# A hybrid attention layer: diagonal copies in scrow, first modulation weights in contiguous blocks, x scaled one K-tile sooner and at first out of PSUM

## The chip, the cores and the metric

The kernel runs on one core of a Trainium2 chip. The core has a matrix engine (TensorE, PE in the profile; its weight loads are the row PEld), a vector engine (VectorE, DVE), a scalar engine (ScalarE, ACT), GpSimd (POOL) and SyncE (SP), which here issues nearly all transfers between the chip's memory and SBUF, the on-chip memory. Products of TensorE land in PSUM, eight banks of 2 KB in each of 128 partitions. The metric is the device time of one execution in microseconds, the median of several runs.

## The reference

One layer with S = 512 tokens and D = 1024 channels, in float32. Cut to what matters:

```python
mod = silu(c) @ w_ada + b_ada                    # c is one vector of 1024
shift, scale, gate = split(mod, 3)
h = rms_norm(x, norm_gain) * (1 + scale) + shift # x is 512 x 1024
proj = h @ w_in                                  # q, k, v, z of head groups A and B, and gates
# group A: sliding-window attention; group B: compressed, selected and window-512 branches
y = concat(o_a * silu(z_a), o_b * silu(z_b)) @ w_out
out = x + gate * y
```

The norm divides each token by the root of its mean square over the 1024 channels. The modulation (`scale`, `shift`) is a product of a vector with a 1024 x 3072 matrix, for each of the 1024 channels.

## The kernel before, in words

**Layout.** x is held transposed, as eight K-tiles of 128 channels by 512 tokens (`xT[0]` to `xT[7]`, in one tile `xTp`). The products with `w_in` run in float32 precision through pairs of rounded parts: h is kept as a high part `hh[k]` and a low part `hl[k]`, the weights as `swh` and `swl`, and each K-tile's product is made of three (`hh` x `swh`, `hh` x `swl`, `hl` x `swh`).

**The head** (lines 312 to 401), all of it with an order written out by hand: inside `in_order` each engine runs its instructions as they stand in the text.

- SyncE issues the transfers: eight K-tiles of x (256 KB each), then for k = 0 to 3 the modulation weights `ada[k]` (1 MB each, `load_ada`), the small `bias` after the first of these, and the weight rows `wst[k]` of the first projection (384 KB each, `load_wst`); then `rest`.
- A tanh of c gives `sc_col`, the silu of c (doubled), a column per block of 128 channels. To have it as a row in all partitions, VectorE makes two diagonal tiles `diag` (128 x 512, line 341), each holding four diagonal blocks, and TensorE multiplies them by ones (line 343). ScalarE copies the two results into `scrow` (line 372) once the sums below are done.
- ScalarE squares each K-tile of x (line 363), VectorE adds the squares up in two groups of four (line 365), and TensorE sums the columns over the partitions (`sums`, line 352). The last tile is done in halves. VectorE then works out the inverse root (`rsqrt`, lines 113 to 120) and TensorE spreads it by transposes into the PSUM tile `rbp` (line 384).
- For K-tiles 0 and 1 the modulation is worked out on TensorE: `mod_pe` (line 252) multiplies the columns of `ada[k]` by c, ScalarE copies the result to `macc` (line 255), `mod_col` sums it and `mod_ab` makes AB, scale and shift of h. For K-tiles 2 to 7 VectorE does it (`mod_rows`, line 242: a multiply with `scrow` and a sum along the row, once for shift, once for scale).
- `fillers` are matmuls whose result nobody reads. The tuple `ND` says how many stand at which place.
- `scaled(k, by)` (line 292) multiplies K-tile k of x by the inverse root on VectorE. Tile 0 takes it out of PSUM (`rbp`) in two halves; the others take it out of `rb`, an SBUF copy that ScalarE makes (line 397). `h_high` makes `hh[k]` and `hf[k]` on ScalarE (line 298; 395 and 398 for tile 0), `h_low` makes `hl[k] = hf[k] - hh[k]` on VectorE (line 301). `weights_high` and `weights_low` split `wst[k]` on ScalarE (line 284) and VectorE (line 287).

**The first projection** (lines 414 to 438): for each K-tile three products (`first_proj`, lines 308 and 309) of 8 matmuls each. After the second of K-tile k, `new_tile(k + 1)` puts the work of the next tile on ScalarE and VectorE. VectorE's order in `new_tile(k)` is `mod_rows(k + 1)`, `h_low(k)`, `scaled(k + 1)`, `weights_low(k + 1)`.

**The remainder** (from 53 us): projections of the other columns, attention of both groups and the output product. Its order comes from generators that are interleaved by cost.

**Buffers.** Tiles of 128 x 512 (`T2`) come out of one pool, small constants out of `con`, PSUM tiles `pj` out of pools of 2 KB banks. The kernel is built with `auto_bufs`: a planner places the tiles in memory after the program's order is known, and may put a tile where another lay whose last reader it takes to be done; the later writer then waits for that reader. It also settles the order of instructions that no `in_order` or `block` fixes. Loads are numbered over eight semaphores, so an issue waits until the transfer eight places before it has landed.

Of the kernel before, what the change touches and what calls it, by code (L numbers as in the profile page):

```python
# [9 lines left out]
F32 = mybir.dt.float32  # L10
# [21 lines left out]
NEAR = 256  # L32
ND = (11, (0, 0, 0, 0, 1, 1, 1, 1), (2, 0), 1, 1, 0, 3)
NR = 4
# [57 lines left out]
def hybrid_layer_kernel(ctx, tc, A, out):  # L92
# [126 lines left out]
    def load_ada(k):  # L219
        t = ada_ring[:, k % NR]  # L220
        if k < PE_MODS:
            ada[k] = t.rearrange("p (a b c) -> p a b c", a=8, b=2)
            for e, n in ((0, 4), (4, 2), (6, 2)) if k == 0 else ((0, 4), (4, 4)):
                SP.dma_start(ada[k][:, e:e + n], A["w_ada_cols"][k][:, e:e + n])
        else:
            ada[k] = t.rearrange("p (a b) -> p a b", a=2)
            for e in range(2):
                SP.dma_start(ada[k][:, e], A["w_ada_rows"][k - PE_MODS][:, e])
# [83 lines left out]
    with in_order(tc) as begun:  # L312
# [8 lines left out]
        for k in range(NR):  # L321
            load_ada(k)
            if k == 0:
                SP.dma_start(bl, A["bias"])
            load_wst(k)
        SP.dma_start(rest, A["rest"])
# [12 lines left out]
        for e in range(2):  # L339
            diag = T2(F32, "diag").rearrange("p (j q) -> p j q", j=4)  # L340
            DVE.tensor_tensor(diag, ident[:, None, :].to_broadcast([128, 4, 128]),
# [35 lines left out]
        DVE.tensor_tensor(prmg[:, 0:8], prm1, prm[:, 24:32], op=OP.mult)  # L377
        DVE.tensor_scalar(prmg[:, 8:16], prm[:, 24:32], 0.5, None, op0=OP.mult)
        fillers(ND[3])
        mod_pe(0, lambda: fillers(ND[4]))  # L380
        fillers(ND[5])
        rbp = ps_pj.tile([128, 512], F32, name="pj")
# [3 lines left out]
        PE.matmul(pl, bl[:, NEAR:NEAR + 40], bl[:, 0:NEAR], start=True, stop=True)  # L386
        fillers(ND[6])
        weights_high(0)
# [10 lines left out]
        weights_low(0)  # L399
        scaled(1, rb)  # L400
        h_low(0)

        def new_tile(k):

            h_high(k, halves if k < 4 else (slice(0, S),))
            if k < 7:
                mod_rows(k + 1, (1,) if k == 1 else (0, 1))
            h_low(k)
            if k < 7:
                scaled(k + 1, rb)  # L410
                weights_high(k + 1)
# [824 lines left out]
def _layout(inp):  # L1236
# [6 lines left out]
    wa = g("w_ada")[0].reshape(8, 128, 3, 8, 128)[:, :, 0:2, 0:PE_MODS]  # L1243
    a["w_ada_cols"] = cc(wa.transpose(3, 1, 0, 2, 4))
    wr = g("w_ada")[0].reshape(D, 3, 8, 128)
# [66 lines left out]
```

## Time and profile before

| | |
|---|---|
| median of 3 runs | 301.43 us (300.99 to 306.27) |
| the profiled execution | 301.42 us |
| its span from first to last instruction | 299.1 us |
| TensorE busy | 292.2 us, 98% |
| TensorE weight loads busy | 254.6 us, 85% |
| VectorE busy | 263.6 us, 88% |
| ScalarE busy | 203.3 us, 68% |
| GpSimd busy | 10.2 us, 3% |
| read from memory, written | 41.74 MB, 2.14 MB |

Times in the rows are counted from the first instruction. A row of the timeline gives start, length, engine, line of the kernel, operation, `output<-input` by the program's names with sizes, and a count; in brackets stands how long the engine had been idle and what ended it. Rows of engines whose name ends in q are those of an engine's instruction queue, transfers' issues among them. A row of the waits gives who waited for whom, the total in us, the number of times and the longest.

### The profile page before, as it was taken

The page shows a single profiled execution, that of the slowest core. Times are in us where ns is not written, and L with a number is a line of the kernel's source. Part 1 is how long each engine was busy: PE and PEld are TensorE (multiplying, and loading weights), DVE is VectorE, ACT ScalarE, POOL GpSimd, SP SyncE. Part 2 cuts the span into 40 slices and gives each one's busy share as a digit, 9 for nine tenths or more (in the row PEclk, how much of TensorE's full clock was granted, in tenths as well). Part 3 has the DMA queues.
Part 4 walks back from the last instruction along what each step waited for, and adds up shares of the span by engine and source line. Part 5 has one row for each costly group of instructions (what it writes and reads, how often), then busy time and mean ns, then how long its engine had stood idle before and what let it go on. Part 6 is the DMA issues. An engine that isn't in the chain of part 4 may idle for free.

```text
span 299.1 us, 6080 instructions
## 1 busy us (share of the span) xinstructions
PE 292.2 (98%) x2179; PEld 254.6 (85%) x2179; DVE 263.6 (88%) x736; ACT 203.3 (68%) x498; POOL 10.2 (3%) x28
## 2 busy tenths in 40 slices
PE   8899999999999999999999999999999999999995
PEld 3678878879989899989877888888888888889995
DVE  4688998999996899899999999988989779599992
ACT  4676656886857666886839575888878769567520
POOL 1000000000000100000000000000000000021210
PEclk9999999999999999999999999999999999999999
DMA  7999975980393766526312211303200220027262
GB/s 263 356 406 358 417 277 178 309 263 2 90 343 104 247 203 216 178 70 233 117 41 71 70 37 35 140 3 114 100 0 2 69 75 0 2 40 191 53 155 92
DMA packets 26649, 44.27 MB, mean 148 GB/s; under 512 B 1867, under 2 KB 17900, under 8 KB 26620
## 3 DMA queue, kind: packets, MB, share of 16 engines
q1 hardware_dynamic: 25612, 42.49, 41.8%
q0 software_dynamic: 864, 1.31, 2.9%
q8 instruction: 17, 0.28, 0.4%
q10 hardware_dynamic: 144, 0.09, 0.1%
q14 instruction: 12, 0.10, 0.1%
HBM read 41.74 MB, written 2.14 MB: 147 GB/s over the span
## 4 chain that ended last, share of the span: by engine, by line
PE 75%; DVE 14%; ACT 5%; issue 3%; DMA 2%; SPq 1%; DVEq 0%; ACTq 0%
PE pj L499 15%; PE pj L489 9%; PE sq L308 8%; PE po L1056 8%; PE pj L1166 6%; PE s L965 5%; PE pt L1037 4%; PE skv L309 4%; PE s L1166 3%; DVE wl L193 3%; PE pt L1023 2%; PE po L499 2%; DMA xTp<-in_xT 2%; DVE kTb L567 2%; PE pt L1166 1%
## 5 line engine op out<-in xcount | busy, mean ns | idle before, releaser
L489 PE MATMUL pj<-wh,hh 128*128 128x256 f32 (+1 forms) x128 | 37.3, 291 | 0.0
L489 PE MATMUL pj<-wl,hh 128*128 128x256 f32 (+1 forms) x128 | 36.7, 286 | 0.0
L489 PE MATMUL pj<-wh,hl 128*128 128x256 f32 (+1 forms) x128 | 36.6, 286 | 0.0
L971 ACT ACTIVATE pp<-pp,nm 128x256 f32<-128x256 f32 (+2 forms) x48 | 29.2, 610 | 5.4 <-DVE nm L967 5.3
L192 ACT ACTIVATE wh<-raw 128x512 fp32r<-128x512 f32 (+1 forms) x40 | 24.8, 637 | 6.6 <-PE pj L499 4.6
L499 PE MATMUL pj<-hh,wh 128*128 128x512 f32 x72 | 28.9, 402 | 0.0
L499 PE MATMUL pj<-hl,wh 128*128 128x512 f32 x72 | 28.9, 401 | 0.0
L499 PE MATMUL pj<-hh,wl 128*128 128x512 f32 x72 | 28.7, 398 | 0.0
L193 DVE TENSOR_TENSOR wl<-raw,wh 128x512 fp32r<-128x512 f32 (+1 forms) x40 | 27.0, 692 | 0.8 <-issue 0.2
L967 DVE CUSTOM_DVE_ANT_0 pp<-s,bias 128x256 f32<-128x256 f32 (+2 forms) x48 | 25.7, 550 | 2.0 <-PE s L965 1.5
L489 PEld LDWEIGHTS pj<-wh,hh 128*128 128x128 f32 x128 | 24.1, 189 | 0.4 <-issue 0.3
L489 PEld LDWEIGHTS pj<-wh,hl 128*128 128x128 f32 x128 | 24.2, 189 | 0.2 <-issue 0.2
L489 PEld LDWEIGHTS pj<-wl,hh 128*128 128x128 f32 x128 | 24.2, 189 | 0.0
L965 PE MATMUL s<-kTb,qs 128*128 128x256 f32 (+2 forms) x96 | 23.6, 349 | 0.0
L1008 DVE TENSOR_SCALAR pp<-pp,rr,grev 128x256 f32<-128x256 f32 (+2 forms) x48 | 21.2, 474 | 0.4
L965 PEld LDWEIGHTS s<-kTb,qs 128*128 128x128 f32 x96 | 16.8, 189 | 2.4 <-issue 0.2
L1038 ACT COPY ptT<-pt 128x384 f32<-128x384 f32 (+1 forms) x32 | 15.5, 525 | 1.9 <-PE pt L1037 1.9
L971 ACT ACTIVATE pa<-pa,nm 128x129 f32<-128x129 f32 x32 | 12.7, 399 | 5.1 <-DVE nm L987 4.7
L1037 PE MATMUL pt<-first,pp 128*128 128x128 f32 x112 | 15.7, 274 | 0.0
L499 PEld LDWEIGHTS pj<-hh,wl 128*128 128x128 f32 x72 | 13.6, 189 | 2.4
L499 PEld LDWEIGHTS pj<-hl,wh 128*128 128x128 f32 x72 | 13.6, 188 | 2.2
L499 PEld LDWEIGHTS pj<-hh,wh 128*128 128x128 f32 x72 | 13.6, 188 | 2.2
(296 smaller groups left out, 835.1 us busy)
## 6 DMA issues: line engine op xcount, KB each, us to landing
ada_ring<-in_w_ada_rows SPq DMA_DIRECT2D x12, 512.0 KB, 7.7
raw<-in_w_cmp SPq DMA_DIRECT2D x8, 512.0 KB, 5.8
raw<-in_w_gate SPq DMA_DIRECT2D x8, 512.0 KB, 4.5
raw<-in_w_o SPq DMA_DIRECT2D x8, 512.0 KB, 3.4
wst_ring<-in_w_qkv_a SPq DMA_DIRECT2D x8, 384.0 KB, 8.2
xTp<-in_xT SPq DMA_DIRECT2D x8, 256.0 KB, 4.5
bias<-line_d SPq DMA_DIRECT2D x8, 256.0 KB, 3.7
raw<-in_w_q_b SPq DMA_DIRECT2D x4, 512.0 KB, 5.0
```

Of the source, the lines that this page charges most:

```text
L192: ACT.activation(wh, src, AF.Copy)
L193: DVE.tensor_tensor(wl, src, wh.bitcast(F32), op=OP.subtract)
L308: PE.matmul(pj_q[tb], lt, w[:, 0:512], start=f, stop=l, skip_group_check=True)
L489: PE.matmul(bank[:, t * n:(t + 1) * n], h[:, tb * 128:(tb + 1) * 128], w[:, k % 2, :], start=k == 0 and m == 0, stop=k == 7 and m == 2)
L499: PE.matmul(bank, w, h, start=k == 0 and m == 0, stop=k == 7 and m == 2)
L965: PE.matmul(ps, qs[8 + 4 * g + r][:, 128 * i:128 * i + 128], kT[br, g][:, hl_, 0:w], start=hl_ == 0, stop=hl_ == 1)
L967: DVE.tensor_tensor_reduce(out=P[:, g, 0:w], in0=ps, in1=bias["b", r, g][:, 512 - w:512], scale=1.0, scalar=3e38, op0=OP.add, op1=OP.min, ...
L971: ACT.activation(P[:, g], P[:, g], AF.Exp, bias=nm[:, g:g + 1], scale=-1.0, accum_out=dn[:, g:g + 1])
L1008: DVE.tensor_scalar(v, v, rr[:, g:g + 1], gates[:, g, br:br + 1], op0=OP.mult, op1=OP.mult)
L1037: PE.transpose(pt[:, b * 128:(b + 1) * 128], P[:, g, b * 128:(b + 1) * 128], ident)
L1056: PE.matmul(o[64 * g:64 * g + 64, 128 * i:128 * i + 128], vb[:, 64 * g:64 * g + 64], sl["T"][g][:, b, :], start=first_of and b == 0, stop= ...
L1166: PE.matmul(parts[g, p], a[:, r, :], b, start=new and r == 0 and m == 0, stop=r == 3 and m == 2, skip_group_check=True)
```

## The change

- The two diagonal tiles are no tiles of their own. They are written into the two halves of `scrow`, in which the result of their products is put later.
- The modulation weights of K-tiles 0 and 1 lie in memory as four blocks of 128 x 512 each, contiguous, 256 KB (before: one row of 8 KB for each partition, of which each transfer took a part). K-tile 0 comes in four transfers of one block (before: three, of 512, 256 and 256 KB), K-tile 1 in two of two blocks.
- The load of `wst[k]` is issued before that of `bias`.
- Of the fillers around `mod_pe(0)` (one ahead, one in its middle) one is left, behind it.
- K-tiles 1 and 2 of x are both scaled ahead of `h_low(0)`, out of `rbp` in PSUM. The copy `rb` stays, for the later tiles.
- In `new_tile(k)` VectorE scales K-tile k + 2 (before: k + 1), ahead of `h_low(k)` (before: behind it).

```diff
-ND = (11, (0, 0, 0, 0, 1, 1, 1, 1), (2, 0), 1, 1, 0, 3)
+ND = (11, (0, 0, 0, 0, 1, 1, 1, 1), (2, 0), 1, 3)
...
             ada[k] = t.rearrange("p (a b c) -> p a b c", a=8, b=2)
-            for e, n in ((0, 4), (4, 2), (6, 2)) if k == 0 else ((0, 4), (4, 4)):
-                SP.dma_start(ada[k][:, e:e + n], A["w_ada_cols"][k][:, e:e + n])
+            parts = t.rearrange("p (a b) -> p a b", a=4)
+            n = k + 1
+            for e in range(0, 4, n):
+                SP.dma_start(parts[:, e:e + n], A["w_ada_cols"][k, e:e + n].rearrange("a p n -> p a n"))
...
             load_ada(k)
+            load_wst(k)
             if k == 0:
                 SP.dma_start(bl, A["bias"])
-            load_wst(k)
...
-            diag = T2(F32, "diag").rearrange("p (j q) -> p j q", j=4)
+            diag = scrow[:, 512 * e:512 * e + 512].rearrange("p (j q) -> p j q", j=4)
...
+        mod_pe(0)
         fillers(ND[3])
-        mod_pe(0, lambda: fillers(ND[4]))
-        fillers(ND[5])
...
-        fillers(ND[6])
+        fillers(ND[4])
...
-        scaled(1, rb)
+        scaled(1, rbp)
+        scaled(2, rbp)
         h_low(0)
...
                 mod_rows(k + 1, (1,) if k == 1 else (0, 1))
+            if k < 6:
+                scaled(k + 2, rb)
             h_low(k)
             if k < 7:
-                scaled(k + 1, rb)
                 weights_high(k + 1)
                 weights_low(k + 1)
...
-    a["w_ada_cols"] = cc(wa.transpose(3, 1, 0, 2, 4))
+    a["w_ada_cols"] = cc(wa.reshape(4, 2, 128, 2, PE_MODS, 128).transpose(4, 0, 2, 1, 3, 5).reshape(PE_MODS, 4, 128, 512))
```

## The prediction

> **What bounds the kernel now.** I read the page first (span, chain), then the busy time by stretch, then the head in order of time, then SyncE's queue, and last the projection stage on VectorE and TensorE.
>
> From the page: the span, and the chain that ended last, by line.
>
> ```profile
> span 299.1 us, 6080 instructions
> PE pj L499 15%; PE pj L489 9%; PE sq L308 8%; PE po L1056 8%; PE pj L1166 6%; PE s L965 5%; PE pt L1037 4%; PE skv L309 4%; PE s L1166 3%; DVE wl L193 3%; PE pt L1023 2%; PE po L499 2%; DMA xTp<-in_xT 2%; DVE kTb L567 2%; PE pt L1166 1%
> ```
>
> The chain's lines are nearly all TensorE's, and the one transfer among them is x (2%), in the head. So what is gained or lost before the first K-tile product travels to the end through engines, and later transfers do not absorb it, unless the stage right behind the head has a bound of its own. The busy time by stretch (columns: span; busy PE, weight load, DVE, ACT, POOL; granted clock; DMA share; GB/s) has such a stage:
>
> ```profile
> 16.26:52.92 36.66, 36.66 (x215) 30.40 (x214) 34.10 (x58) 23.69 (x41) 0.21 (x2) 1.00 0.87 325
> 52.92:299.00 246.08, 241.28 (x1893) 216.51 (x1892) 220.04 (x646) 170.96 (x442) 9.27 (x21) 1.00 0.36 110
> ```
>
> In the projection (16.26 to 52.92 us) VectorE is busy for 34.10 of 36.66 us, nearly as long as TensorE. Behind it TensorE idles only 4.80 of 246.08 us. The head in order of time (start, length, engine, line, instruction):
>
> ```profile
> 7.40 0.63 ACT L363 ACTIVATE sq<-xTp 128x512 f32<-128x512 f32 x1 [1.63 <-PE sq L343]
> 8.45 1.75 ACT L363 ACTIVATE sq<-xTp 128x512 f32<-128x512 f32 x4
> 9.10 2.35 DVE L365 TENSOR_TENSOR sacc<-sacc,sq 128x512 f32<-128x512 f32 x4 [0.35 <-ACT sq L363]
> 11.17 1.05 PE L352 MATMUL pj<-ones,sacc 128*128 128x1 f32 x8
> 14.22 0.62 PE L384 MATMUL pj<-first,n_y 128*128 128x128 f32 x4 [0.30 <-DVE prm L376]
> 15.60 1.10 ACT L395 ACTIVATE hh<-xTp,AB 128x256 fp32r<-128x256 f32 x2 [0.50 <-DVE AB L278]
> 16.26 0.50 PE L308 MATMUL sq<-swh,hh 128*128 128x512 f32 x1
> ```
>
> ScalarE stands idle for 1.63 us before the fourth Square, until a matmul that reads a diagonal copy ends. Nothing that this Square computes comes from there, so its result must take the memory of a diagonal tile. The later Squares and VectorE's adds run back to back behind it, then the column sums (11.17), the root, its transposes (14.22), the first h (15.60) and the first product (16.26).
>
> **The removed wait.** Without it, x sets the pace. SyncE's queue shows when its tiles land, since each issue waits for the transfer eight places ahead:
>
> ```profile
> SPq L224 <- DMA xTp<-in_xT: 0.6, 2, 0.3
> 6.27 0.37 SPq L324 DMA_DIRECT2D raw<-in_bias  x1
> 7.66 1.02 SPq L224 DMA_DIRECT2D ada_ring<-in_w_ada_cols  x2
> 8.98 0.33 SPq L232 DMA_DIRECT2D wst_ring<-in_w_qkv_a  x1
> 12.91 0.33 SPq L232 DMA_DIRECT2D wst_ring<-in_w_qkv_a  x1
> 13.29 1.05 SPq L228 DMA_DIRECT2D ada_ring<-in_w_ada_rows  x2
> ```
>
> x tile 3 is there at 6.27, tile 5 at 7.66, tile 6 at about 8.35 (the second issue of the 7.66 row), tile 7 at 8.98. So the fourth Square can start at 6.3 in place of 7.40, and the sixth, the first of the 8.45 row, at 7.68, as its tile lands: 0.77 us sooner. Its add then starts at 8.33 (9.10 now). The four adds follow each other about 0.8 us apart (9.10 row: two whole and two half ones in 2.35 us); the last Squares wait for tiles 6 and 7, which are there 0.7 to 0.9 us before their adds want them. So the sums start at 10.40, the transposes at 13.45, h at 14.83 and the first product at 15.49: **0.77 us**. TensorE's own fillers before the sums run out at about the same time, so 0.70 is possible. If the Square takes another busy buffer instead, the gain is smaller (a rival below). The diagonal copies write as many elements as before into scrow, which ScalarE overwrites only after the sums: nothing.
>
> **Is the rest of the head there 0.77 us sooner?** A filler, the products with the first modulation weights, the first weight rounding, and one stretch (last column GB/s):
>
> ```profile
> 12.96 0.39 PE L333 MATMUL skv<-zero 128*128 128x512 bf16 x1
> 13.28 0.64 PE L252 MATMUL pj<-ada_ring,scz 128*32 128x256 f32 x8
> 14.27 0.83 ACT L284 ACTIVATE swh<-wst_ring 128x768 fp32r<-128x768 f32 x1
> 8.00:10.00 2.00, 1.64 (x13) 1.39 (x12) 1.49 (x3) 2.00 (x6) 0.00 (x0) 1.00 0.96 232
> ```
>
> The last piece of these weights lands at 12.91 (the issue there waits for it). Even unchanged, the last products (four of the eight in 0.64 us) would end at 13.2, the one filler left (0.39) at 13.6, and the transposes would be 0.15 us late against 13.45. But from 8 to 10 us, as the strided weights begin, the transfers move 232 GB/s, against 380 of x, which comes in contiguous blocks of 256 KB (262,144 bytes between the landings at 7.66 and 8.35). If the new blocks of the same size run like x, 2.0 x (1 - 232/380) = 0.78 us comes back and the last piece lands at about 12.1: no delay. I take this, since x is the same form; the other end is 0.15 us. The fourth piece costs one more issue (0.33 us) in a queue that waits for landings anyway. [...]
>
> Weight rows wst 0 land at 14.01 now (second issue of the 13.29 row). They no longer stand behind the bias. The rounding (0.83) must end by 14.83, so even 14.01 costs only 0.04. The bias lands behind them instead, 393,216 bytes or an estimated 1 us later at 380 GB/s, less the 0.78; it landed by 13.29, since an issue that needs its place went out then, and its matmul follows the transposes, at 14.1 or later. One filler less takes work off TensorE only; the granted clock is 1.00 in every stretch.
>
> **The projection.** The order there matters, since VectorE is full:
>
> ```profile
> 17.35 0.81 ACT L398 ACTIVATE hf<-xTp,AB 128x512 f32<-128x512 f32 x1
> 17.48 0.69 DVE L292 TENSOR_TENSOR xTp<-xTp,rb 128x512 f32<-128x512 f32 x1 [0.78 <-ACT rb L397]
> 18.05 0.84 ACT L284 ACTIVATE swh<-wst_ring 128x768 fp32r<-128x768 f32 x1
> 19.80 1.28 DVE L242 CUSTOM_DVE_ANT_0 ada_ring<-ada_ring,scrow,first 128x1024 f32<-128x1024 f32 x1
> 21.00 0.15 DVE L277 TENSOR_TENSOR AB<-pj,first 128x1 f32<-128x1 f32 x1
> 23.36 0.84 ACT L284 ACTIVATE swh<-wst_ring 128x768 fp32r<-128x768 f32 x1
> 25.57 1.28 DVE L242 CUSTOM_DVE_ANT_0 ada_ring<-ada_ring,scrow,first 128x1024 f32<-128x1024 f32 x1
> 32.59 0.69 DVE L301 TENSOR_TENSOR hl<-hf,hh 128x512 fp32r<-128x512 f32 x1
> 33.19 0.69 DVE L292 TENSOR_TENSOR xTp<-xTp,rb 128x512 f32<-128x512 f32 x1
> 33.79 0.96 DVE L287 TENSOR_TENSOR swl<-wst_ring,swh 128x768 fp32r<-128x768 f32 x1
> 34.66 1.29 DVE L242 CUSTOM_DVE_ANT_0 ada_ring<-ada_ring,scrow,first 128x1024 f32<-128x1024 f32 x1
> 37.13 0.70 DVE L301 TENSOR_TENSOR hl<-hf,hh 128x512 fp32r<-128x512 f32 x1
> 22.18 0.39 PE L308 MATMUL sq<-swh,hh 128*128 128x512 f32 x1
> 26.34 0.39 PE L308 MATMUL sq<-swh,hh 128*128 128x512 f32 x1
> 42.43 0.50 PE L308 MATMUL sq<-swh,hl 128*128 128x512 f32 x1
> 48.49 0.50 PE L308 MATMUL sq<-swh,hh 128*128 128x512 f32 x1
> ACT kr L800 <- DVE gsig L799: 1.8, 1, 1.8
> ```
>
> One tile costs TensorE 4.16 us (22.18 to 26.34) and VectorE 4.54 (32.59 to 37.13: low part 0.60, scaling 0.60, low weights 0.87, modulation rows 2.47). So later tiles go at VectorE's pace and TensorE waits for low parts and for h. From 42.43 it has one product of tile 5 and two whole tiles left, 4.16 x (1/3 + 2) = 9.71 us; from 48.49 one tile, to 52.65. That is 10.22 us, with 0.51 of waiting.
>
> *Does scaling out of PSUM start sooner?* VectorE waits 0.78 us for ScalarE's copy rb (17.48 row). The copy stays, and stands ahead of the two scalings in the program. The last row above is from the waits: ScalarE's copy kr waits 1.8 us for VectorE's gsig, though both only read, other columns of one PSUM tile (L799, L800). Reads of a PSUM tile by two engines are put one behind the other here, so I expect the 0.78 us wait to stay, for the same copy. [...]
>
> All below in today's clock less 0.77. Scalings at 16.71 and 17.31 (0.60 each, as in SBUF; two 256-column halves out of PSUM would cost up to 0.14 more each), the low part of tile 0 at 17.91 (hf is done at 17.39), low weights of tile 1 at 18.52, its cover 18.12 for swh being past, the first modulation row at 19.39, and AB of tile 1 at 20.6 instead of 21.00: **0.4 us of the 0.77**. TensorE waits there for the rest. Everything that ScalarE makes of it is 0.4 sooner: swh of tile 2 ends at 23.8 (now 24.20). But scaling 3 now fits into the time in which VectorE waits for hf of tile 1, so low weights 2 start at 23.84 and the next modulation rows at 24.71, not 25.57: **0.86 sooner**, and so for every later tile, at the same 4.54. In each, the low part now comes after the scaling, 0.60 later: 0.26 sooner net. So the third product of tile 5 starts at 42.17. From there nothing holds TensorE: h of tiles 6 and 7 waits no longer for a scaling, scalings 6 and 7 are through, and the 0.51 us goes too. Sum: 0.26 + 0.51 = **0.77 us** at 52.65. The new order by itself gains nothing; it lets the head's gain through.
>
> The profiled execution took 301.42 us (299.1 and 2.3 around it), the median of the runs is 301.43: prediction 301.42 - 0.77 = 300.65, say **300.7 us**. Unknowns: -0.15 (weights), -0.07 (fillers), -0.28 (PSUM operand), together down to 0.27 gained: 301.15. On the other side the 4.80 us of idle TensorE behind 52.92 may fall otherwise, since a planner orders and packs the remainder. I allow 0.7 either way.
>
> **Rivals.**
> - *VectorE reads beside ScalarE's copy.* For it: both only read. Against: the kr row. The scalings follow the low weights at 15.85; AB of tile 1 comes the full 0.77 sooner, low weights 2 at 23.47 and modulation rows at 24.34, 1.23 sooner; gain 1.23 - 0.60 + 0.51 = 1.14: 300.3 us.
> - *The change doesn't do what it says: the fourth Square keeps a wait*, on another buffer. Once the adds of Squares 2 and 3 are done (by 5.69 + 1.48 = 7.17, from the row below) a Square could start, so 0.2 us or nothing is gained: 301.2 to 301.4.
>
> ```profile
> 5.69 1.48 DVE L365 TENSOR_TENSOR sq<-sq 128x512 f32<-128x512 f32 x2
> 8.80 1.05 PE L352 MATMUL pj<-ones,sq 128*128 128x1 f32 x8 [0.36 <-DVE sq L365]
> ```
>
> - *A worse buffer, slower.* With two tiles fewer in use, the planner may give the sixth Square the buffer of the first sums, which TensorE reads until the column sums end (8.80 row). These would run from about 8.3 to 9.35. The sixth Square then starts at 9.35 instead of 8.45 and the whole chain is 0.9 us late: 302.3 us. It decides against the change once the release lies after 8.45. For it: this is how today's wait arose. Against: buffers of Squares 2 to 4 are free sooner.
>
> **Numbers.** Forecast 0.60, concurrent reads 0.12, wait kept 0.12, worse buffer 0.06, a reshuffled remainder beyond 0.7 us 0.10. The forecast's own range is 299.9 to 301.5; with the rivals, the range is 299.7 to 301.8, which leaves out the worse buffer and the far reshuffles. Two per cent, about what a measurement of this kernel can tell from no change, is 6 us: 295.4 or 307.5. No case reaches it; I keep 0.01 and 0.02 for a reshuffle: 0.97 within.
>
> **What would show it.** Fourth Square at about 6.3 with no wait for L343, sums at 10.4, first product at 15.5; 8 to 10 us at 380 GB/s or more; the first scaling out of PSUM still waiting for rb; AB of tile 1 only 0.4 sooner; VectorE without a gap before the low part of tile 1; last product near 51.9. Wrong would be: no gap before the first scaling, a new wait in the Squares, or a first product at 15.5 whose gain is gone by 52 or behind it.

## The result and the profile after

The changed kernel takes **305.1 us** (median of 5 runs, 304.43 to 306.14) against 301.43 for the kernel before: ratio 1.0129, 95% interval 1.0104 to 1.0154. It is slower by 3.7 us, where 300.7 had been forecast. The profiled execution after took 304.43 us, the lowest of its runs, with a span of 301.8 us; that of before took 301.42, with 299.1. So the two traces hold 2.7 us of span to explain; 0.3 us more lies outside the spans (2.6 us against 2.3), and some 0.7 us of the medians' difference lies between runs and is in no trace. In the changed kernel most line numbers are 2 or 3 higher.

The page after, span and chain by line:

```profile
span 301.8 us, 6071 instructions
PE pj L502 15%; PE po L1059 6%; PE pj L1169 6%; PE s L968 5%; PE pt L1040 4%; PE s L1169 3%; PE pt L1026 1%; PE pt L1169 1%; DVE wl L193 1%; PE s L684 1%; DVE qs L553 1%; PE po L1065 1%; PE s L941 1%; ACT pp L948 1%; ACT pp L974 0%; DVE qn L542 0%
```

The chain no longer reaches back to the head: the first projection (L310, L311) and x are gone from it. In order of time it begins at 143.7 us, behind a multiply that has a new wait (below). The head in order of time, after:

```profile
5.93 0.63 ACT L365 ACTIVATE sq<-xTp 128x512 f32<-128x512 f32 x1 [0.20 <-DMA xTp<-in_xT]
7.00 0.63 ACT L365 ACTIVATE sacc<-xTp 128x512 f32<-128x512 f32 x1 [0.45 <-DMA xTp<-in_xT]
10.48 1.05 PE L354 MATMUL pj<-ones,sacc 128*128 128x1 f32 x8 [0.21 <-DVE sacc L367]
13.46 0.62 PE L385 MATMUL pj<-first,n_y 128*128 128x128 f32 x4 [0.93 <-DVE prm L378]
14.78 1.09 ACT L396 ACTIVATE hh<-xTp,AB 128x256 fp32r<-128x256 f32 x2 [1.00 <-DVE AB L280]
15.43 0.53 PE L310 MATMUL sq<-swh,hh 128*128 128x512 f32 x1
```

No Square waits for a matmul any more, and the first product starts at 15.43 in place of 16.26: **0.83 us** sooner, 0.77 forecast. The fifth Square (7.00) has a small new wait instead, for x. By stretch, before and then after (columns as in the prediction):

```profile
16.00:52.90 36.90, 36.90 (x216) 30.38 (x214) 34.34 (x58) 23.93 (x42) 0.19 (x2) 1.00 0.87 326
52.90:92.00 39.10, 38.57 (x287) 34.38 (x286) 36.09 (x109) 28.95 (x80) 1.52 (x7) 1.00 0.61 192
140.00:146.00 6.00, 6.00 (x45) 5.60 (x44) 5.81 (x10) 5.32 (x11) 0.00 (x0) 1.00 0.40 143
```

```profile
8.00:10.00 2.00, 2.00 (x18) 2.00 (x18) 1.39 (x2) 1.93 (x5) 0.00 (x0) 1.00 1.06 409
16.00:52.90 36.90, 35.23 (x209) 29.43 (x208) 33.48 (x58) 23.49 (x39) 0.44 (x3) 1.00 0.84 317
52.90:92.00 39.10, 38.02 (x279) 33.75 (x278) 36.27 (x106) 29.65 (x81) 1.26 (x5) 1.00 0.58 187
140.00:146.00 6.00, 5.28 (x45) 5.07 (x45) 4.63 (x8) 3.62 (x7) 0.00 (x0) 1.00 0.38 150
```

From 8 to 10 us, while the last of x and the first of the contiguous weights arrive, the transfers move 409 GB/s (232 before). But TensorE, which had no gap in the projection, now idles 1.67 us there (36.90 - 35.23), 0.55 us more from 53 to 92 us, and 0.72 us in the six from 140 us on. The projection after, in order of time:

```profile
16.65 1.28 DVE L294 TENSOR_TENSOR xTp<-xTp,pj 128x512 f32<-128x512 f32 x2 [0.71 <-ACT rb L398]
18.20 0.85 ACT L286 ACTIVATE swh<-wst_ring 128x768 fp32r<-128x768 f32 x1 [0.87 <-PE pj L254]
19.81 0.96 DVE L289 TENSOR_TENSOR swl<-wst_ring,swh 128x768 fp32r<-128x768 f32 x1 [1.27 <-ACT raw L431]
21.89 0.15 DVE L279 TENSOR_TENSOR AB<-pj,first 128x1 f32<-128x1 f32 x1
22.91 0.50 PE L310 MATMUL sq<-swh,hh 128*128 128x512 f32 x1 [1.36 <-ACT hh L300]
42.71 0.68 DVE L303 TENSOR_TENSOR hl<-hf,hh 128x512 fp32r<-128x512 f32 x1
43.44 0.50 PE L310 MATMUL sq<-swh,hl 128*128 128x512 f32 x1
53.25 0.39 PE L502 MATMUL po<-hh,wh 128*128 128x512 f32 x1
```

ScalarE's rounding of the weights of tile 1 (18.20) waits 0.87 us for a modulation matmul, VectorE's low weights (19.81) wait 1.27 us, AB of tile 1 comes at 21.89 (21.00 before), and TensorE stands idle for 1.36 us until h of tile 1. All later tiles come late with it: the low part of tile 5 (42.71) holds its product to 43.44, 1.01 us later than before (42.43, shown in the prediction). The matmul behind the projection starts at 53.25. The low part of tile 5 and that matmul in the trace before:

```profile
41.68 0.70 DVE L301 TENSOR_TENSOR hl<-hf,hh 128x512 fp32r<-128x512 f32 x1
52.76 0.39 PE L499 MATMUL po<-hh,wh 128*128 128x512 f32 x1
```

From the product at 43.44 on TensorE needs 9.81 us to the end of the projection (10.33 from 42.43 before), so the tail got 0.52 us shorter, and still 0.83 us of gain have become 0.49 us of loss: 1.32 us went in the projection. From there, the starts of the same ScalarE instructions in the two traces lie 0.39 us apart at 75 us, 1.36 at 92, 1.26 at 140 and 2.33 from 145 to 286 us, and the span 2.7. So there are two more steps, of about 0.9 us (53 to 92) and 1.1 us (at 141), and 0.4 us at the very end. The step at 141 us: VectorE's multiply with the last gate weights, and SyncE's issues of their two halves; before, then after.

```profile
135.54 2.20 SPq L174 DMA_DIRECT2D raw<-in_w_gate  x2
140.08 1.28 DVE L724 CUSTOM_DVE_ANT_0 raw<-raw,scrow,first 128x1024 f32<-128x1024 f32 x1
```

```profile
136.65 1.23 SPq L174 DMA_DIRECT2D raw<-in_w_gate  x2
142.41 1.29 DVE L727 CUSTOM_DVE_ANT_0 raw<-raw,scrow,first 128x1024 f32<-128x1024 f32 x1 [1.10 <-DMA raw<-in_w_gate]
```

Before, the halves are issued 1.87 us apart (2.20 less the second's 0.33), and the first has landed when VectorE comes. After, they are issued 0.90 us apart (1.23 less 0.33), the first lands at 142.4, 5.7 us after its issue, and VectorE waits 1.10 us. And the end, by the last row of the chain in order of time (start, length), before and after:

```profile
294.53 1.43 PE pj L1166 x12
```

```profile
296.84 1.43 PE pj L1169 x12
```

From the last product to the end of the span: 299.1 - 295.96 = 3.14 us before, 301.8 - 298.27 = 3.53 after.

### The profile page after: what moved, and what is told of

Its sections match the earlier page's. It is cut to its first block, busy times and chain, and to the rows that moved or that the text cites. A ratio compares the mean times of both kernels' runs of the same rounds, so it can differ in the third digit from the quotient of the medians.

```text
span 301.8 us, 6071 instructions
## 1 busy us (share of the span) xinstructions
PE 291.0 (96%) x2177; PEld 254.7 (84%) x2178; DVE 263.7 (87%) x736; ACT 205.0 (68%) x498; POOL 10.2 (3%) x28
## 4 chain that ended last, share of the span: by engine, by line
PE 44%; DVE 5%; ACT 2%; issue 0%; ACTq 0%
PE pj L502 15%; PE po L1059 6%; PE pj L1169 6%; PE s L968 5%; PE pt L1040 4%; PE s L1169 3%; PE pt L1026 1%; PE pt L1169 1%; DVE wl L193 1%; PE s L684 1%; DVE qs L553 1%; PE po L1065 1%; PE s L941 1%; ACT pp L948 1%; ACT pp L974 0%; DVE qn L542 0%
## 5 line engine op out<-in xcount | busy, mean ns | idle before, releaser
L1027 ACT COPY ptT<-pt 128x256 f32<-128x256 f32 (+1 forms) x28 | 12.8, 458 | 4.3 <-PE pt L1026 3.8
```

## The experiments

Every run is timed beside the kernel before on the same chip. "Shift" is how much later (+) or sooner (-) the same ScalarE instruction starts than in the trace of before, at about 22, 53, 92, 141, 145 and 286 us.

| run | before, this (us) | ratio, 95% interval | shift at 22 / 53 / 92 / 141 / 145 / 286 |
|---|---|---|---|
| e1 | 301.56, 302.91 | 1.0036 [0.9999, 1.0072] | not usable |
| e2 | 301.56, 301.81 | 1.0023 [1.0007, 1.0038] | -0.76 / -0.78 / -0.82 / -0.94 / -0.10 / -0.03 |
| e3 | 301.56, 303.69 | 1.0068 [1.0048, 1.0088] | -0.49 / -0.89 / +0.04 / +0.20 / +1.08 / +0.96 |
| e4 | 301.56, 302.94 | 1.0064 [1.0029, 1.0099] | +0.14 / -0.25 / +0.64 / +0.54 / +1.42 / +1.40 |
| e5 | 301.73, 303.46 | 1.0064 [1.0032, 1.0095] | -0.64 / -1.00 / -0.14 / -0.02 / +0.94 / +0.94 |
| e6 | 301.73, 301.74 | 1.0022 [0.9987, 1.0057] | -0.91 / -0.91 / -0.91 / -0.63 / -0.59 / -0.58 |
| e7 | 301.73, 301.51 | 1.0001 [0.9970, 1.0031] | +0.13 / +0.12 / +0.11 / +0.38 / +0.93 / +0.94 |
| e8 | 301.73, 301.43 | 1.0016 [0.9979, 1.0053] | -0.35 / -1.49 / -1.51 / -1.63 / -0.59 / -0.58 |
| e9 | 301.75, 301.68 | 0.9998 [0.9971, 1.0025] | -0.11 / -0.12 / -0.11 / +0.18 / +0.19 / +0.19 |
| e10 | 301.75, 300.84 | 0.9969 [0.9943, 0.9996] | -0.43 / -1.51 / -1.50 / -1.49 / -1.15 / -0.87 |
| e11 | 301.75, 300.95 | 0.9984 [0.9965, 1.0003] | -0.62 / -1.75 / -1.76 / -1.82 / -0.85 / -0.94 |
| e12 | 301.75, 302.75 | 1.0034 [1.0021, 1.0047] | +1.04 / +1.05 / +1.05 / +1.07 / +1.11 / +1.11 |
| e13 | 301.66, 303.93 | 1.0086 [1.0043, 1.0129] | at 53: +1.67, 92: +2.57, 141: +2.47, 145: +2.48 |
| e14 | 301.66, 300.32 | 0.9944 [0.9907, 0.9981] | at 53: -0.83, 92: -0.86, 141: -0.97, 145: -0.97 |
| e15 | 301.66, 301.33 | 0.9993 [0.9969, 1.0017] | at 141: -1.33, 145: -0.08 |
| e16 | 301.66, 300.67 | 0.9966 [0.9923, 1.0008] | at 53: -1.71, 92: -1.70, 141: -1.69, 145: -1.68 |
| e17 | 301.49, 299.21 | 0.9917 [0.9885, 0.9949] | -0.69 / -1.83 / -1.82 / -1.84 / -1.84 / -2.02 |

In the profiles of e1, e7, e13 and e14 TensorE's granted clock falls to 0.50 in the head (last section), so only differences of shifts inside such a profile, and its medians, are used.

### Which part makes the wait at tile 1?

The change with the scaling put back as it was (e1); the same with fixed places for the split weights (e2); the whole change with fixed places, for `hf` too (e3).

```diff
# e1, against the changed kernel
-        scaled(1, rbp)
-        scaled(2, rbp)
+        scaled(1, rb)
...
-            if k < 6:
-                scaled(k + 2, rb)
             h_low(k)
             if k < 7:
+                scaled(k + 1, rb)
# e2 = e1 and these; e3 = the changed kernel, these and hf_ring
+swh_ring = stp.tile([128, 3, 768], F32R, name="swh_ring")
+swl_ring = stp.tile([128, 2, 768], F32R, name="swl_ring")
-        ws[k] = (stp.tile([128, 768], F32R, name="swh", bufs=3), stp.tile([128, 768], F32R, name="swl", bufs=3))
+        ws[k] = (swh_ring[:, k % 3], swl_ring[:, k % 2])
+hf_ring = stp.tile([128, 2, S], F32, name="hf_ring")
-        hf[k] = T2(F32, "hf")
+        hf[k] = hf_ring[:, k % 2]
```

> The changed kernel with the scaling put back: tile 1 scaled by ScalarE's copy of the root, each later tile scaled behind the low part of the one before it. The diagonal's buffer, the contiguous first weights and the load order stay. Theory B (the loss sits in buffers that the compiled program shares): the second tile's split weights still share the buffer of the first tile's, so its low half still waits for the product of tile 0 (start near 19.8 us, AB of tile 1 near 21.9); the head keeps its 0.8 us; the h buffers of the later tiles are apart again; the projection ends 0.3 to 0.9 us later than before's 51.80; behind it every engine's order is that of before, so the rest is before's: 301.4 + 0.3 to 0.9 = 301.7 to 302.3 us. Rival S (the new order inside the tile costs the time, the buffers nothing): the head's 0.8 us comes through, 300.6 us. Rival L (the loss comes from the loads or from where the gate weights land): as slow as the changed kernel, 304 to 305 us.

> As the run with the old scaling, but the split weights have buffers of their own (three for the high halves, two for the low halves, kept to the end of the projection), so nothing of tile 1's weights waits for a product of tile 0. Theory B: low half of tile 1's weights starts near 18.1 us, AB of tile 1 at 20.4 to 20.7 (before 21.00), projection ends 0.4 to 0.9 us sooner than before's 51.80, the rest as before: 300.5 to 301.0 us, some 1.0 to 1.5 us less than its sister. Rival S: the same 300.6 us, but then no less than its sister. Rival V (VectorE's work for each tile takes the head's gain whatever the buffers do): 301.4 us.

> The changed kernel whole, but with buffers of their own for the split weights (three and two) and two alternating buffers for the full-precision h. Theory B with theory O (the other order of the work behind the projection costs about 2 us by itself): the waits for the product of tile 0 and for the low part before go, the projection ends near 51.0 to 51.5 us (changed kernel 52.30, before 51.80), the order behind it stays that of the changed kernel and keeps its 1.3 us at 83 to 92 us and part of the 1.1 us at 141 us: 302.5 to 303.5 us. Theory B alone (the buffers are all of it): 300.5 us. Rival S (the order inside the tile): 304 to 305 us as the changed kernel, with the projection's end near 52.3.

e1: 302.91 us, so putting the scaling back takes off 2.2 of the 3.7 us, and something else holds the rest. e2: 301.81, 1.1 less by the memory places alone. Both are slower than expected, by 0.6 and 0.8 us; in e2 the rest of the gain goes at 141 us and in a longer end (below). The stage at tile 1 in e2:

```profile
17.29 0.83 ACT L288 ACTIVATE swh_ring<-wst_ring 128x768 fp32r<-128x768 f32 x1
18.16 0.96 DVE L291 TENSOR_TENSOR swl_ring<-wst_ring,swh_ring 128x768 fp32r<-128x768 f32 x1
20.23 0.15 DVE L281 TENSOR_TENSOR AB<-pj,first 128x1 f32<-128x1 f32 x1
```

The two waits are gone, AB of tile 1 is at 20.23, 0.77 us sooner than before, and the head's gain arrives whole at 53 us (-0.78) and 141 us (-0.94). The compiled programs say which memory it is: in the changed kernel the low weights of tile 1 were put in the place of those of tile 0, which products of tile 0 still read, and the columns of c that `mod_pe` reads overlap `swh` of tile 1. Before, the low weights alternated between two places. The trace's row names another releaser for the 1.27 us (a ScalarE copy that had ended); e12, below, has the wait with a product as its releaser.

e3, 303.69: with fixed places the projection goes as the prediction had worked it out.

```profile
20.57 0.15 DVE L282 TENSOR_TENSOR AB<-pj,first 128x1 f32<-128x1 f32 x1
42.06 0.50 PE L313 MATMUL sq<-swh_ring,hl 128*128 128x512 f32 x1
```

AB of tile 1 is at 20.57 (20.6 forecast), the third product of tile 5 starts at 42.06 (42.17), and at 53 us e3 is 0.89 us ahead (0.77). But it keeps 2.1 us of loss, all of it behind the projection.

Which part moved those places? The new scaling alone in the kernel before (e4); the change with the old order of loads (e5); diagonals, contiguous weights and fillers alone (e6); the diagonals alone (e7); and e7 with the exchanged loads (e12).

```diff
# e5, against the changed kernel; e12 is e7 with the exchange made
             load_ada(k)
-            load_wst(k)
             if k == 0:
                 SP.dma_start(bl, A["bias"])
+            load_wst(k)
```

> The kernel before with the scaling one tile sooner and the first two out of PSUM, nothing else: the diagonal's buffer, the strided weights and the load order are before's. Theory B with O: the fourth Square waits its 1.6 us again, the split weights stay apart, the full-precision h of all later tiles lies in one buffer and waits up to 0.4 us a tile for the low part; the projection ends within 0.5 us of before's 51.80; the order behind it is that of the changed kernel and costs 1.3 to 2.3 us: 302.7 to 304.0 us. Rival F (the order behind the projection costs nothing, what is lost there comes from a late front): 301.2 to 301.7 us.

> The changed kernel with one line put back: the bias is loaded ahead of the first projection weights again. In the compiled program the second tile's split weights then have buffers of their own (their low half waits for no product, their high half not for the last modulation product); the full-precision h of the later tiles still lies in one buffer, and the order behind the projection stays that of the changed kernel. Theory B+O: the projection ends 1.2 to 1.5 us sooner than in the changed kernel (near 50.9 to 51.1), the remainder as there: 3.9 - 1.4 = 2.5 us over before, 303.6 to 304.1 us. Rival H (the single h buffer is the larger part, since it waits in every tile): 304.5 to 305 us. Rival L (what order the two loads land in does not matter): as the changed kernel, 305 us.

> The change without its new scaling and without its new load order: the diagonal in its result's buffer, the contiguous first weights and the two filler products fewer stay. In the compiled program every buffer that the projection and the raw weights use, and every engine's order behind the projection, is then that of before. Theory B+O+G (G: the gate weights' loads behind 135 us cost 0.8 us where their two halves are issued 0.9 us apart as in the run with own buffers, and nothing where they are issued 1.9 us apart as before): the head's 0.8 us comes through to the end: 300.6 to 300.9 us (before 301.5). Rival A (the second half of the span takes the head's gain back whatever the buffers, since a load there lands at its own time): a step up at 141 us in the profile and 301.4 to 301.8 us, as the run with old scaling and own buffers.

> The kernel before with the diagonal in its result's buffer and nothing else. Theory B: the fourth Square waits no more, the modulation weights land as late as before (12.9 us), which takes nothing off the gain because the products of the root come later still; projection ends 0.7 to 0.8 us sooner, the rest as before: 300.7 to 300.9 us. Rival (the weights' landing holds the first projection product): 301.1 to 301.4 us.

> The run with the diagonal alone (301.41 us), with one more edit: the first projection weights are loaded ahead of the bias. Strided modulation weights, old scaling. In the compiled program the second tile's low half then shares the first tile's buffer, and its high half the place of the modulation's columns; nothing else of the buffers and orders differs from that run. Theory B: tile 1's low half waits for the product of tile 0 (1.3 us on VectorE), the projection ends 1.2 to 1.5 us later than in that run, and the rest follows: 302.5 to 302.9 us. Rival (the exchange of the two loads harmed only together with the new scaling): 301.3 to 301.7 us.

The exchange of two loads alone costs about 1.2 us: e12 is 1.00 us behind its kernel before, e7 0.22 ahead of its own. In e12 the rows have the waits and the lateness of the changed kernel, and the low weights' wait is put down to a product (L309):

```profile
18.34 0.85 ACT L284 ACTIVATE swh<-wst_ring 128x768 fp32r<-128x768 f32 x1 [0.86 <-PE pj L252]
19.96 0.96 DVE L287 TENSOR_TENSOR swl<-wst_ring,swh 128x768 fp32r<-128x768 f32 x1 [1.75 <-PE skv L309]
22.04 0.16 DVE L277 TENSOR_TENSOR AB<-pj,first 128x1 f32<-128x1 f32 x1
```

e5, without the exchange, is 1.7 us slow in place of 3.7, as are e3 and e4 roughly (2.1 and 1.4): all three come out of the projection ahead of the kernel before (table, at 53 us), and what is left goes behind it (next sections). e6 and e7 missed: the head's 0.91 us is in e6's trace at 53 us, but the medians of both are those of before within 0.3 us.

### What is lost behind the projection?

From 53 to 92 us, e3, e4, e5 and the change lose 0.9 us each (table), e2 and e6 nothing; the first group has the new scaling. Its last two tiles are the ones that stand at the projection's end, so e8 is e3 with the scaling carried ahead only up to tile 5:

```diff
-            if k < 6:
+            if k < 4:
                 scaled(k + 2, rb)
             h_low(k)
             if k < 7:
+                if k > 4:
+                    scaled(k + 1, rb)
```

> The changed kernel with own buffers for split weights and h, and the scaling one tile sooner only up to tile 5 (tiles 6 and 7 are scaled behind the low part, as before). In the compiled program the order of ScalarE and VectorE behind the projection is then that of before. Theory O (the other order costs 1.1 us between 57 and 92 us): projection ends 0.8 to 0.9 us sooner than before's 51.80, as in the run of the change with own buffers; the stretch to 92 us adds nothing; the gate step at 141 us (0.85 us) stays, since the raw weights' buffers are still not before's: 1.1 us less than that run's 303.7, 302.4 to 302.7 us. Rival (the order is innocent; what is lost to 92 us comes from the early front meeting loads that land at their own time): 303.4 to 303.8 us.

301.43 us, 2.3 us less than e3 and more than expected. From 57 to 75 us, waits of e3 that e8 doesn't have:

```profile
PEld pt L567 <- ACT wh L192: 0.7, 1, 0.7
PEld pj L495 <- ACT pa L977: 0.6, 1, 0.6
PE pj L495 <- ACT ptT L1030: 0.5, 1, 0.5
```

and the stretch by engine, e3 and then e8:

```profile
57.00:75.00 18.00, 16.75 (x111) 14.56 (x110) 17.00 (x43) 12.91 (x34) 0.38 (x2) 1.00 0.42 140
```

```profile
57.00:75.00 18.00, 17.47 (x122) 15.38 (x122) 16.94 (x43) 12.99 (x34) 0.38 (x2) 1.00 0.44 148
```

TensorE idles 0.72 us less in e8, as little as in the kernel before (17.47 us busy there too), because the planner orders the work there differently. From 55 us on the traces have two orders of ScalarE's, VectorE's and TensorE's instructions, equal within each group down to the last one: one in the kernel before and the thirteen runs without the scaling carried through to tile 7, another in the changed kernel, e3, e4, e5 and e13. The 0.93 us that e3 loses from 53 to 92 us are gone (-1.49 to -1.51 in e8). Why scaling two tiles later makes the planner choose another order is not known.

And e8 comes out of the projection 0.60 us sooner than e3 (-1.49 against -0.89). The low part of tile 5 and its product, in e3 and in e8:

```profile
41.33 0.68 DVE L306 TENSOR_TENSOR hl<-hf_ring,hh 128x512 fp32r<-128x512 f32 x1
42.06 0.50 PE L313 MATMUL sq<-swh_ring,hl 128*128 128x512 f32 x1
```

```profile
40.26 0.68 DVE L306 TENSOR_TENSOR hl<-hf_ring,hh 128x512 fp32r<-128x512 f32 x1
41.53 0.39 PE L313 MATMUL sq<-swh_ring,hl 128*128 128x512 f32 x1
```

In e3 this low part stands behind the scaling of tile 7, and TensorE's product starts as it ends (41.33 + 0.68 = 42.01). In e8 it is there 1.07 us sooner, and the product no longer waits for it.

### Does the new scaling gain anything, and what does one more transfer cost?

e9 is e6 with the first weights in three pieces instead of four; e10 is e9 with the new scaling for tiles 1 to 4; e11 has it up to tile 5, with the `hf` ring.

```diff
# e9, e10 and e11, against the changed kernel
-            n = k + 1
-            for e in range(0, 4, n):
+            for e, n in ((0, 2), (2, 1), (3, 1)) if k == 0 else ((0, 2), (2, 2)):
...
# e10, against the changed kernel
-            if k < 6:
+            if k < 3:
                 scaled(k + 2, rb)
...
+                if k > 3:
+                    scaled(k + 1, rb)
```

> As the run of the diagonal and the weights, but the first modulation weights come in three contiguous pieces instead of four, so that SyncE issues as many loads and stores as in the kernel before and the last store reports on the semaphore that the end of the program waits for last. Theory T (with one store more the last one reports on a semaphore that is waited for first, and the waits for the others follow it: 0.4 us between the landing of the last store and the end, 1.33 against 0.94 us): 0.4 us less than its sister's 301.65, 301.1 to 301.4 us, with 0.85 to 0.95 us between the last landing and the end. Rival (those 0.4 us are chance): 301.5 to 301.8 us.

> The run before it with the new scaling added for tiles 1 to 4 (the first two out of PSUM, tiles 3 and 4 ahead of the low part); tiles 5 to 7 are scaled as before. In the compiled program the order behind the projection and the buffers of the last gate weights are those of before. Theory B+O+G: the new order inside the tile is harmless or a small gain: projection ends 0.9 to 1.5 us sooner than before's 51.80, the two halves of the last gate weights are issued 1.9 us apart, the step at 141 us is 0 to 0.6 us: 300.5 to 301.3 us, no more than the run before it. Rival S (the new order costs time by itself): 0.3 us or more over the run before it, 301.5 to 302 us.

> As the run before it, but the full-precision h has two alternating buffers and the scaling is ahead to tile 5; the last gate weights lie in other buffers again, whose loads wait for other readers. Theory B+O+G: projection ends 1.4 to 1.6 us sooner than before's 51.80 (as with own buffers for everything); the order behind it is before's; the step at 141 us follows the distance between the two halves' issues, 0.9 us if they are 0.9 us apart and at most 0.3 us if they are 1.9 us apart: 300.2 to 300.6 us with a wide distance, 301.0 to 301.4 us with a narrow one. Rival F (a load that lands at its own time takes back whatever the front gains): 301.2 to 301.6 us with a step that is as large as the front's gain, whatever the distance.

e9 gave 301.68, no gain: a miss. Its end is as short as before (about 3.1 us from the last product). Over all profiles the end takes about 3.1 us where SyncE issues 111 transfers (before, e4, e7, e9 to e12, e15 to e17) and 3.5 to 3.9 us where it issues 112 (after, e1 to e3, e5, e6, e8, e13, e14). But in its head x came late, by the timeline:

```profile
7.73 0.63 ACT L364 ACTIVATE sacc<-xTp 128x512 f32<-128x512 f32 x1 [1.09 <-DMA xTp<-in_xT]
```

The fifth Square waits 1.09 us for tile 4, which took most of the gain. e10 and e11 show that the new order is worth something: 300.84 and 300.95 us, 0.8 and 0.7 less than e9. In e10's trace the first product starts 0.79 us sooner than before (15.47) and the projection ends 1.51 us sooner, so 0.72 us come from the order, and nothing of it is lost up to 141 us. Carried through to tile 7 it gives much less in the projection: the same difference is 0.10 us in e3, 0.02 in e4 and 0.01 in e5.

### The step at 141 us

In e11 the two halves of the last gate weights are issued 0.59 us apart, and its multiply still waits 0.99 us for the first. The wait is 0.87 to 1.28 us in the eight profiles where the halves go out within 0.6 to 0.9 us (after, e2, e3, e4, e5, e8, e11, e15), and 0 to 0.57 in the seven where it is 1.8 to 1.9 us (before, e1, e6, e7, e9, e10, e12). Ahead of these issues SyncE's queue stands behind one load, by the waits of the changed kernel from 131 to 137 us:

```profile
SPq L930 <- DVE n_t L115: 4.8, 1, 4.8
```

It is a load of the attention's `bias` that waits 4.8 us for its buffer (4.8 in the kernel before, too). So in e13 (the change), e14 (e8), e16 (e10) and e17 (e11) the gate weights are queued ahead of it; e15 is e11 once more.

```diff
+    gate_dma = []
...
+            if (g, h) == ("gate3", 1):
+                gate_dma.append([i for i in tc.nc.cur_bb.bb.instructions if i.engine == SP.engine][-1])
...
-                if kind == "a" and i == 0 and r >= 2:
-                    load_bias_b(r - 2)
+                if (kind, r, br, i) == ("a", 2, 0, 0):
+                    load_bias_b(0)
+                if (kind, r, br, i) == ("b", 0, 2, 1):
+                    with in_order(tc, {SP.engine: gate_dma[0]}, (SP.engine,)):
+                        load_bias_b(1)
```

> The changed kernel with one edit far behind the projection: the last two loads of the bias (256 KB each) are put on SyncE's queue behind the loads of the last gate weights instead of ahead of them, so the gate weights no longer queue behind a load that waits for a buffer. All engines' orders and all buffers but the bias's are those of the changed kernel. Theory G (the step at 141 us is VectorE's wait for the first half of these weights, set by the loads around it): the first half is issued near 131 us and lands before 137, the wait of 1.10 us at 141 us goes and nothing takes its place: 305.1 - 1.1 = 303.7 to 304.2 us. Rival F (the time lost there comes back as another wait, on the bias or on the later weights): 304.8 to 305.4 us.

> The run with own buffers and the old order behind (301.31 us; wait of 1.06 us at 141 us), with the gate weights' loads ahead of the bias's. Theory G: the projection's gain of 1.5 us goes through to the end: 300.1 to 300.5 us. Rival F: 301.1 to 301.5 us.

> A repetition of the run with own h buffers and the scaling ahead to tile 5 (300.94 us, wait of 0.99 us at 141 us) as the base for the next one, on the same chip: 300.7 to 301.1 us by either theory.

> The run with the scaling ahead to tile 4 (300.83 us, wait of 0.37 us at 141 us), with the gate weights' loads ahead of the bias's. Theory G: 0.3 to 0.5 us less, 300.3 to 300.6 us. Rival F: 300.7 to 301.0 us.

> What the runs so far found to help, in one kernel: diagonal in its result's buffer, three contiguous pieces of the first modulation weights, bias ahead of the first projection weights as before, scaling ahead up to tile 5 only, two alternating buffers for the full-precision h, the last gate weights ahead of the bias's last loads. Theory B+O+G: projection ends 1.3 to 1.7 us sooner than before's 51.80, no wait at 141 us, 0.9 us between the last landing and the end: 299.8 to 300.3 us. Rival F (each cure brings a wait of its own, as the run with own h buffers had at 141 us): 300.6 to 301.2 us.

The step between 141 and 145 us is gone in all four (e13 +2.47 to +2.48, e14 -0.97 both, e16 -1.69 to -1.68, e17 -1.84 both), and nothing takes its place; e15, without the move, has it (-1.33 to -0.08) and takes 0.4 us more than e11, which it repeats. The medians follow: e13 is 1.2 us faster than the change, e14 1.1 faster than e8. e16 gains only 0.2 on e10, which had little of the wait (0.37 us); its 300.67 us lies between what the two theories gave. e17 holds what has paid: the diagonals in `scrow`, contiguous weights in three pieces, the old order of loads, the scaling ahead up to tile 5 with its own `hf` places, and the gate weights first. It takes **299.21 us** against 301.49, ratio 0.9917 [0.9885, 0.9949], 0.6 us less than the best that was expected, and beats both kernels:

```profile
span 297.1 us, 6044 instructions
```

## Why the prediction was wrong

It failed at three steps: AB of tile 1, the allowance for the remainder, and the "one more issue". All its steps, one by one:

**The removed wait: right.** Sums at 10.48 (10.40 forecast), transposes at 13.46 (13.45), h at 14.78 (14.83), first product at 15.43 (15.49). Left out was tile 4 of x: the working gave the landings of tiles 3, 5, 6 and 7. Before, the wait covered tile 4; now the fifth Square waits for it, 0.45 us in the changed kernel and 1.09 in e9. So the gain of the head depends on when x lands: in e10, whose loads are those of e9, the same Square waits for it 0.19 us. It is right for the traces; in the times it hardly shows. The medians of e6, e7 and e9, which have this gain and no new scaling, lie within 0.2 us of those of the kernel before. The clock doesn't explain it: over the executions whose mean granted clock was 0.998 or more, e7 is 0.18 and e9 0.25 us below the kernel before, e6 0.15 above. In e6's trace 0.91 us of gain at 53 us are 0.58 at 286, and its end is 0.4 us longer; in e9's, x was late. Whether that is all of it was not tried and stays open.

**The rest of the head: right on the weights, wrong on "costs nothing" and "one more issue (0.33 us)".** The stretch from 8 to 10 us moved 409 GB/s, where 380 was taken, and their products run at once, ahead of the transposes, which wait for VectorE (0.93 us). The fourth piece cost nothing at its place but 0.4 us at the end of the program (3.53 against 3.14 us). The exchange of bias and `wst` was worked out only for when each lands. It cost about 1.2 us (e12), through the planner: with another order of loads it puts tiles in other places.

**The projection: wrong at "AB of tile 1 at 20.6".** It came at 21.89. The working had the low weights of tile 1 at 18.52, "its cover 18.12 for swh being past", and asked only when their input is ready, not whose memory they are written into. `swh` waited 0.87 us and the low weights 1.27 us for readers of other tiles in their places. e2, with its own places, shows AB at 20.23 under the old scaling, and e3 at 20.57 under the new one, so the rest of the working of this stage held. The wait for `rb` stayed, 0.71 us, as forecast.

**"The new order by itself gains nothing": right for the change as it was made.** In the projection it gave 0.10, 0.02 and 0.01 us (e3, e4, e5). Nor did anything hold TensorE from the third product of tile 5 on, as forecast: it ran from 43.44 to 53.25 without a gap, only 1.27 us later than the 42.17 that the working gave, which is the lateness of AB. What the working didn't ask is what scaling fewer tiles ahead would give: up to tile 4 it gains 0.7 us in the trace and 0.8 in the medians (e10, e9), since the low parts of tiles 4 and 5 then no longer stand behind a scaling.

**The remainder, "0.7 either way": mis-sized, and this is the larger part of the miss.** The forecast amounts to a span of 298.3 us, 3.5 us less than the trace. Of these the projection has 1.3 us, the end 0.4 and the remainder 1.8: two steps, of 0.9 us (53 to 92 us) and 1.1 us (at 141 us), added to one side. The first goes with the scaling of the last two tiles (e8), the second goes where the gate weights are queued sooner (e13, e14, e16, e17). The row on which both could have been put was there: behind 52.92 us TensorE idled only 4.80 of 246 us, so a reordering could gain 4.80 us at most and lose without such a bound.

**The rivals.** VectorE beside ScalarE's copy and a wait kept in the Squares are refuted by the rows at 16.65 (a wait of 0.71 us for `rb`) and 5.93 (the fourth Square waits 0.20 us for x alone). "A worse buffer, slower" named the right kind of mechanism, in the Squares and at 0.9 us; it happened at tile 1 instead, where the projection lost 1.32 us in the trace and the exchange alone 1.2 in the medians. "A reshuffled remainder beyond 0.7 us", at 0.10, also came true. With both, the sum for the profiled span is: -0.83 in the head, +1.32 in the projection, +0.87 to 92 us (0.49 to 1.36), -0.10 to 140 us, +1.07 at 141 us, +0.37 at the end, together +2.7 us.

**What would show it** named the sign that came: a first product at 15.5 whose gain is gone by 52 us.

## What to carry to other kernels

Where a planner places tiles and orders work after the program is written, price an edit by its side effects too: compare the memory places and the instruction order of both compiled programs, and ask of each moved tile who reads its place last. An exchange of two loads that seemed free cost about 1.2 us here, and pinning places (e2, e8) or carrying a reorder only as far as it has slack behind it (e10, e17) brought back most of a loss of 3.7 us; with one load moved besides, it became a gain of 2.3. A wait that is removed was also the cover of what lands during it (here x, which then held the fifth Square for 0.45 us in the changed kernel and 1.09 in e9): look up the landing of every tile in that stretch.

## What the hardware showed that was not expected

**Halves issued close together, and a late landing.** The first half of the last gate weights lands 4.5 to 5.1 us after its issue in the seven profiles where the second follows 1.8 to 1.9 us later, and 5.5 to 5.9 us after it in the eight where it follows 0.6 to 0.9 us later. The two go together without an exception there, and VectorE comes for it some 4.6 us after the issue (140.08 - 135.54 = 4.54 in the kernel before). That the closeness is the cause was not tried by itself, since e13, e14, e16 and e17 move the whole load.

**TensorE's granted clock fell to 0.50 in the head of four profiles,** e1, e7, e13 and e14; in the others it stayed at 1.00 there. e7, by stretch:

```profile
6.00:8.00 2.00, 1.40 (x6) 0.57 (x4) 1.74 (x3) 1.79 (x3) 0.00 (x0) 1.00 1.06 409
8.00:10.00 2.00, 2.00 (x18) 2.00 (x18) 1.66 (x3) 1.92 (x6) 0.00 (x0) 1.00 1.03 331
10.00:12.00 2.00, 2.00 (x16) 1.27 (x18) 1.01 (x6) 0.51 (x2) 0.00 (x0) 0.79 1.05 410
12.00:14.00 2.00, 2.00 (x17) 0.30 (x9) 1.26 (x9) 0.00 (x0) 0.00 (x0) 0.50 1.03 415
14.00:16.00 2.00, 2.00 (x15) 1.36 (x12) 0.95 (x5) 1.40 (x3) 0.00 (x0) 0.86 1.03 406
```

Against 1.00 the clock of e7 lacks (0.21 + 0.50 + 0.14) x 2.00 = 1.70 us from 10 to 16 us; at the 0.50 of the row from 12 to 14 us that would be 3.4 us, an estimate. The same rows of e13 (0.96, 0.50, 0.69) and e14 (0.80, 0.50, 0.85) lack 1.70 us too. Those of e1 (1.00, 0.90, 0.50) lack 1.20 us; over its whole span of 303.8 us e1's mean clock of 0.989 lacks 3.3 us, against 1.8 in e7 (0.994 of 300.0). Eight products with modulation weights took 1.08 us in e7 (0.64 before), and e7's trace is 0.13 us behind that of before at 22 us, where e6's is 0.91 ahead. In e7's rows TensorE is busy for 1.40 of the two us before 8 and throughout from 8 on. What set the fall off was not tried and stays open.
